# Three z projections by seven block products instead of eight, and norm weights spread by TensorE

## The chip, the cores and the metric

The kernel runs on one core of one Trainium2 chip. The metric is the device time of one execution in microseconds (us), the median of three runs. A profile is one more execution, taken by the hardware profiler. Engines are named as the profile names them: PE is TensorE's matmul, PEld its weight load, DVE is VectorE, ACT ScalarE, POOL GpSimd, and SP the engine whose queue issues every DMA of this kernel.

## What is computed

One layer of a decoder trunk with two token mixers side by side, on 1024 tokens of width 1024. The part that the change touches is the norm of the input and one of the eight parts of the input projection, z_s:

```python
h = rms_norm(x, norm_w)
proj = h @ w_in
q, k, v, z_a, xbc, z_s, dt_raw, gate_logits = jnp.split(proj, SPLIT_POINTS, axis=-1)
...
xbc = jax.nn.silu(causal_depthwise_conv(xbc, conv_w, conv_b))
dt = jax.nn.softplus(dt_raw.astype(jnp.float32) + dt_bias.astype(jnp.float32))
y_s = ssd_chunked(xs, dt, A, Bm, Cm, d_skip)
y_s = gated_group_rms_norm(y_s, z_s, ssd_norm_w)        # y * silu(z), four groups of 512
```

z_s is 2048 wide, 512 columns for each of four groups, and is needed when that group's scan runs.

## The kernel before

**Numbers.** Every fp32 operand of a large matmul is split into a high and a low part of the matmul's own type (ACT copies the high part, DVE or POOL subtracts it from the original), and a product is three matmuls: high x high, high x low, low x high (steps3). hH and hL hold the two parts of the normed input, with its width on the partitions.

**Front.** x comes in eight tiles of 128 tokens. prep_h squares and sums a tile on ACT, takes the root on POOL, scales it on DVE by the root and by the norm's weights (nwb, loaded by two DMAs that write the same row into all 128 partitions), and transposes it on PE; h_evac makes hH and hL. For tokens 512 to 1023, form_evac also makes four sums of quarters of the input (ft), which the seven-product scheme uses.

**The units.** The projection's parts are computed in a fixed order (ORDER1): z of group 0, dt, z of group 1, then the conv and gate parts in pairs, with z of groups 2 and 3 among them, then the attention heads. A conv or gate unit (front_pair) takes the 1024 x 256 weights and the 1024 x 1024 input each as 2x2 blocks and computes the four blocks of the result with seven block products instead of eight; sums of weight blocks are made on POOL (pair_splits), sums of results on DVE (front_sum). Such a product has 12 matmuls of 512 columns. The z units are plain (ssd_proj_z, proj_tok): for each of 8 token tiles, 8 blocks of 128 x 512 weights, three matmuls each, with the input stationary and the weights moving; z_evac puts silu on the result (ACT) and stores it.

**dt.** dt_proj computes 64 result columns, copies them to SBUF (dtraw), transposes them (ptdt) and then runs softplus on DVE and ACT over many small operations (tv).

**What sets the order.** The program is written by a planner (Plan): tasks are Python generators, each instruction has an assumed cost, and what comes next in assumed time is written next. On the chip every engine goes through its own instructions in that order and waits where an operand isn't there; the assumed costs only set the order. Buffers are counted: four raw weight tiles (raws), nine split weight tiles (ws), 16 of 2 KB per partition for everything between (mids), eight PSUM banks (trs). The scan (ssd_chunk) is spread among the units at one chunk per 20 us (PACE) at least. Weights are loaded (w_loads) and split (w_splits) in the order of the units, as far ahead as buffers allow.

Lines of the profile: L199 is every matmul, L208 every transpose, L225 every ACT operation, L233 a two-operand operation on DVE or POOL, L241 one with a scalar, L246 and L250 one-operand ones, L254 a DMA.

Of the kernel before, what the change touches and what calls it, by code (L numbers as in the profile page):

```python
# [8 lines left out]
F32 = mybir.dt.float32  # L9
# [6 lines left out]
P = 128  # L16
# [11 lines left out]
C_B = C_XBC + 2048  # L28
C_C = C_B + 512
C_ZS = 7168  # L30
# [109 lines left out]
def tile_hybrid_layer(ctx: ExitStack, tc: tile.TileContext, x, norm_w, w_in, q_norm_w, k_norm_w,  # L140
# [22 lines left out]
    cv_d = dram.tile([3072, S], F32, name="cv_d")  # L163
    z_d = dram.tile([GROUPS, S, 512], F32, name="z_d")
    t_d = dram.tile([12, 2, P, S], F32, name="t_d")

# [44 lines left out]
    def pe_done():  # L211
        return pl.t + 0.2
# [136 lines left out]

    CONV = (16, 20, 0, 2, 4, 6, 18, 22, 8, 10, 12, 14)  # L350
    ORDER1 = [("z", 0), ("dt", 0), ("z", 1)]
    for i in range(12):
        ORDER1 += [("c", CONV[i])] + ([("g", i - 1)] if i % 2 else [])
        if i in ZF:
            ORDER1.append(("z", ZF[i]))
    FPAIRS = [i for i in ORDER1 if i[0] in "cg"]
    ORDER1.append(("setup", 0))
    for h in range(HEADS):
        ORDER1.append(("h", h))
        if h in ZH:  # L360
            ORDER1.append(("z", ZH[h]))

    wlist = []
    for kind, i in ORDER1:
        if kind in "cg":
            wlist.append(pair_w(w_in, 0, (C_XBC if kind == "c" else C_GATE) + i * P))
        elif kind != "setup":
            wlist += att_w(i) if kind == "h" else wide_w(w_in, C_ZS + i * 512) if kind == "z" else block_w(w_in, KB, C_DT, SH)
# [11 lines left out]
    def w_loads(lo, hi):  # L380
        for i in range(lo, hi):
# [10 lines left out]
            if isinstance(wlist[i], list):  # L392
                ks = yield from pl.get(raws, 4)
                raw = [rpool.tile([P, 4, P], F32, tag="raw", name=f"rawf{i}{q}") for q in range(4)]
                raw_of[i] = (raw, ks, [load(raw[q], wlist[i][q // 2][:, :, q % 2 * P:(q % 2 + 1) * P]) for q in (0, 1, 2, 3)])
                continue
            while i >= len(wlist) - 2 * KB and "filled" not in ready:
# [26 lines left out]
    def w_splits():  # L424
        for i in range(len(wlist)):
# [5 lines left out]
            if isinstance(wlist[i], list):  # L431
                yield from pair_splits(*raw_of.pop(i), "G" if i < NFRONT else "V")
                continue
            k = yield from pl.get(ws)
# [17 lines left out]
    def pair_splits(raw, ks, at, eng):  # L452
# [33 lines left out]
        raws.give(ks[2], t)  # L486
        raws.give(ks[3], max(t, t22))

    def pairs_splits(raw, ks, at):
# [142 lines left out]
    def prep_h(t):  # L632
# [22 lines left out]
        pts = []  # L655
        nt = []
        for i in range(2):
# [400 lines left out]

    cv_at, z_at, ssd_n = {}, {}, {}

    def front_form(f, i):
# [5 lines left out]
    def front_pair(kind, b, last):  # L1067
# [6 lines left out]
        cell = {"kc": (yield from pl.get(mids)), "x": x, "ks": ks}  # L1074
        step = conv_step if kind == "c" else gate_step
        for n, (f, p) in enumerate(ORDER):
# [17 lines left out]
            w_done(ids[n])  # L1094
            pl.spawn(step(b, p, into[p], cell), pe_done())

# [10 lines left out]

    def gate_out(row, h, src, o, k, at):
        yield at
        at = act(o, src, AF.Tanh, at, scale=0.5)  # L1110
        t = at
        yield at
        at = load(gt_d[row * P:(row + 1) * P, h * 512:h * 512 + 512], o, at)
        mids.give(k, at)
        return t

    def gate_step(b, p, ps, cell):
        at = pe_done()
# [3 lines left out]
        elif p == 2:  # L1122
            k = yield from pl.get(mids)
            t = yield from gate_out(b, 0, ps, midt(name="go"), k, at)
            trs.give(kx, t)
        elif p == 4:
            c = cell["c"]
            at = tt(c, c, ps, ALU.add, max(at, cell["u", 7][2]))
            trs.give(ky, at)
            yield from gate_out(b + 1, 0, c, c, cell["kc"], at)  # L1130
        else:
# [5 lines left out]
            if p == 3:  # L1137
                trs.give(kz, at)
            yield from gate_out(b + (p == 5), 1, u, u, k, at)

# [83 lines left out]
    def ssd_core(g):  # L1224
# [16 lines left out]
        need = [(b, h) for b in [16 + g, 20 + g] + list(range(g * 4, g * 4 + 4)) for h in range(2)]  # L1241
        while any(cv_at.get(i, INF) > pl.t for i in need) or any((g, t) not in z_at for t in range(NT)):
            yield pl.t + 0.5
# [513 lines left out]
    def bulk():  # L1757
# [3 lines left out]
        for kind, i in ORDER1:  # L1761
            if kind in "cg":
                yield from front_pair(kind, i, (kind, i) == FPAIRS[-1])
            elif kind in step:
                yield from step[kind](i)
            else:
                yield from dt_proj() if kind == "dt" else att_setup()
        pl.spawn(fill())
# [5 lines left out]

    kn = [mids.take() for _ in range(2)]
    nwb = [midt(name=f"nwb{i}") for i in range(2)]

    def start():
        load_x(0)
        for i in range(2):  # L1780
            load(nwb[i], norm_w[:, i * 512:i * 512 + 512].partition_broadcast(P).rearrange("p a d -> p (a d)"))
        yield from w_loads(0, 4)
# [8 lines left out]
        while len(h_at) < 2 * NT:  # L1791
            yield pl.t + 1.0
        for k in kn:
            mids.give(k, pl.t)

    def rest():
# [35 lines left out]
```

## Time and profile before

| | us |
|---|---|
| median of three runs | 1624.73 (1622.62 to 1625.15) |
| the profiled execution | 1625.04 |
| its span | 1623.3 |
| PE busy in it | 1589.2 (98%) |
| DVE, ACT, POOL busy | 1088.5, 915.1, 706.9 |

The span reaches from the first to the last instruction of the profile; the rest of an execution's time lies around it. Busy time says how long an engine had something in work. An engine that is busy nearly all the time sets the time; what the others do costs only where it waits for them. In the timeline a row has the start, the duration, the engine, the line, the operation, its output and inputs, their size, and a count where rows were merged; a bracket says how long the engine stood idle before and what it waited for. Matmuls overlap: a row's duration is longer than the distance to the next one, and the distance is what counts. In the forms, 128x256 is partitions by columns.

### The profile page before, as it was taken

What the parts mean: (1) busy time and instruction counts of PE and PEld (TensorE: products, weight loads), DVE (VectorE), ACT (ScalarE), POOL (GpSimd) and SP (SyncE); (2) the same over time, 40 slices, a digit from 0 to 9 for tenths busy, and PEclk for the clock granted to TensorE, in tenths of its full rate; (3) what the DMA queues carried; (4) which work ended last, traced back from release to release, by engine and by line L of the source; (5) the groups of instructions that cost most, each with busy time, mean ns of one, the idle gap of its engine ahead of it and who ended that gap; (6) DMA issues with size and microseconds to landing.
All of it is one profiled execution on the core that took longest, in us unless ns stands there. A gap on an engine that the chain in (4) does not pass through costs nothing.

```text
span 1623.3 us, 24344 instructions
## 1 busy us (share of the span) xinstructions
PE 1589.2 (98%) x8010; PEld 1330.2 (82%) x8010; DVE 1088.5 (67%) x2011; ACT 915.1 (56%) x2215; POOL 706.9 (44%) x847
## 2 busy tenths in 40 slices
PE   7999999999999999999989999999999999999999
PEld 5788888888788888887878888887887888888887
DVE  7836567537782576876767777876556577798831
ACT  7534447445563475786766777776666565352220
POOL 4315445334542543546475746464756433323000
PEclk9999999999999999999999999999999999999999
DMA  6213343533453461425163432433426397698941
GB/s 210 92 55 105 112 145 111 168 101 114 125 168 107 121 183 61 131 79 182 40 207 128 145 90 85 120 101 103 155 80 206 99 310 253 207 340 254 317 153 65
DMA packets 223804, 236.47 MB, mean 146 GB/s; under 512 B 15285, under 2 KB 155326, under 8 KB 223678
## 3 DMA queue, kind: packets, MB, share of 16 engines
q1 hardware_dynamic: 223678, 234.93, 45.6%
q8 instruction: 63, 1.03, 0.3%
q14 instruction: 63, 0.52, 0.1%
HBM read 164.48 MB, written 70.39 MB: 145 GB/s over the span
## 4 chain that ended last, share of the span: by engine, by line
PE 73%; DVE 3%; ACT 2%; POOL 2%; DMA 2%; issue 1%; SPq 0%; POOLq 0%; DVEq 0%; ACTq 0%
PE pma L199 18%; PE py L199 6%; PE pmz L199 5%; PE po L199 5%; PE pO L199 4%; PE pz L199 4%; PE px L199 4%; PE sc L199 4%; PE av L199 4%; PE fYc L199 3%; PE fXc L199 2%; PE pg L199 2%; PE pa L208 2%; PE fZc L199 2%; PE fYg L199 1%; PE pS L199 1%
## 5 line engine op out<-in xcount | busy, mean ns | idle before, releaser
L199 PE MATMUL pma<-w,hH 128*128 128x512 f32 x1024 | 345.2, 405 | 6.0 <-POOL w L233 5.4
L199 PEld LDWEIGHTS pma<-w,hH 128*128 128x128 f32 x1024 | 188.6, 189 | 40.9 <-POOL w L233 6.6
L199 PE MATMUL pma<-w,hL 128*128 128x512 f32 x512 | 206.8, 404 | 0.0
L199 PE MATMUL pmz<-w,hH 128*128 128x512 f32 x512 | 164.1, 398 | 0.7 <-ACT hH L225 0.7
L233 POOL TENSOR_TENSOR rawf<-rawf,rawf 128x512 f32<-128x512 f32 x54 | 71.6, 1326 | 166.4 <-DVE wp L233 87.8
L225 ACT ACTIVATE p<-p,nm 128x256 f32<-128x256 f32 (+7 forms) x128 | 98.6, 773 | 33.6 <-DVE nm L831 32.9
L225 ACT ACTIVATE w<-raw 128x512 fp32r<-128x512 f32 (+1 forms) x122 | 75.1, 626 | 75.0 <-DMA raw<-in_w_in_dram 28.7
L199 PEld LDWEIGHTS pmz<-w,hH 128*128 128x128 f32 x512 | 96.5, 190 | 20.6 <-ACT hH L225 1.1
L199 PEld LDWEIGHTS pma<-w,hL 128*128 128x128 f32 x512 | 96.8, 189 | 16.4
L233 POOL TENSOR_TENSOR w<-raw,w 128x512 fp32r<-128x512 f32 (+1 forms) x38 | 51.3, 1351 | 134.5 <-ACT w L225 120.7
L199 PE MATMUL fYc<-ft,wp 128*128 128x512 f32 x432 | 106.5, 392 | 0.7 <-DVE fu L233 0.7
L199 PE MATMUL pmz<-w,hL 128*128 128x512 f32 x256 | 101.4, 396 | 0.0
L199 PEld LDWEIGHTS fYc<-ft,wp 128*128 128x128 f32 x432 | 81.1, 189 | 17.9 <-DVE fu L233 1.1
L225 ACT ACTIVATE wp<-rawp 128x512 fp32r<-128x512 f32 x72 | 44.2, 626 | 84.1 <-POOL rawp L233 23.9
L233 DVE TENSOR_TENSOR wp<-rawf,wp 128x512 fp32r<-128x512 f32 x72 | 59.1, 837 | 34.7 <-ACT wp L225 34.7
L233 DVE TENSOR_TENSOR w<-raw,w 128x512 fp32r<-128x512 f32 (+1 forms) x84 | 65.1, 782 | 23.5 <-ACT w L225 23.3
L225 ACT ACTIVATE ab<-ab,nac 128x128 f32<-128x128 f32 x256 | 78.4, 392 | 1.7 <-POOL ab L1234 1.5
L199 PEld LDWEIGHTS av<-v,at 128*128 128x128 f32 x576 | 72.8, 191 | 6.5 <-ACT at L225 2.6
L265 POOL TENSOR_TENSOR rs<-rs,mhalf 128x4 f32<-128x4 f32 (+1 forms) x71 | 75.4, 1062 | 5.9
L225 ACT ACTIVATE wp<-rawf 128x512 fp32r<-128x512 f32 x108 | 65.9, 626 | 20.0 <-POOL rawf L233 16.4
L199 PE MATMUL av<-v,at 128*128 128x128 f32 x576 | 75.1, 275 | 1.7 <-ACT at L225 1.7
L831 DVE CUSTOM_DVE_ANT_0 p<-sc,maskb 128x512 f32<-128x512 f32 (+3 forms) x128 | 72.1, 584 | 6.2 <-PE sc L199 3.9
(299 smaller groups left out, 4217.8 us busy)
## 6 DMA issues: line engine op xcount, KB each, us to landing
raw<-in_w_in_dram SPq DMA_DIRECT2D x104, 256.0 KB, 3.6
rawf<-in_w_in_dram SPq DMA_DIRECT2D x72, 256.0 KB, 3.7
ab<-act_d SPq DMA_DIRECT2D x32, 512.0 KB, 4.9
cv_d<-cv SPq DMA_DIRECT2D x48, 256.0 KB, 2.1
t_d<-ts SPq DMA_DIRECT2D x24, 512.0 KB, 3.1
z_d<-zs SPq DMA_DIRECT2D x32, 256.0 KB, 2.0
xr<-cv_d SPq DMA_DIRECT2D x32, 256.0 KB, 3.0
zc<-z_d SPq DMA_DIRECT2D x32, 256.0 KB, 3.0
```

The source lines that it names most:

```text
L199: nc.tensor.matmul(o, lhsT=lhsT, rhs=rhs, start=start, stop=stop, **kw)
L208: nc.tensor.transpose(out=o, in_=i, identity=ident if idn is None else idn)
L225: nc.scalar.activation(o, i, f, **kw)
L233: (nc.vector if eng == "V" else nc.gpsimd).tensor_tensor(out=o, in0=a, in1=b, op=op)
L265: nc.gpsimd.tensor_tensor(out=dst, in0=dst, in1=mhalf[:, 0:cols], op=ALU.pow)
L831: nc.vector.tensor_tensor_reduce(out=p[:, j:e], in0=sc[i][:, 0:e - j], in1=maskb[:, S - n + j:S - n + e], scale=-1.0, scalar=nms[i - 1] if ...
```

## The change

z of groups 1, 2 and 3 is computed with seven products of 2x2 blocks too; group 0 stays plain. The new unit (tok_unit) keeps z's layout, tokens on the partitions: the input's blocks are stationary, four tiles of 128 tokens each, and the weights' blocks, 128 x 256, move. A weight block has two tiles (kp) with two blocks of 128 rows each; so a product has 2 x 4 x 2 x 3 matmuls of 256 columns. Two token tiles share a PSUM bank, and each of the three accumulators (x, y, z) has two banks. Results are summed by DVE into 128 x 512 tiles, get silu on ACT and are stored with two tokens tiles each. tok_splits makes the sums of the weights on POOL and the splits on ACT, DVE and POOL; it takes four raw tiles and four of the shared ones (mids) for one unit.

The order of the units is now a string, with z2 ahead of c4 (before, behind g4) and z3 ahead of c8 (before, behind g8). PACE is 21 instead of 20. The norm's weights are loaded as two rows of one partition; a matmul with a column of ones (K = 1) spreads each over 128 partitions into a PSUM bank, which it keeps until all of x is scaled.

```diff
-PACE = 20
+PACE = 21
...
-ZF, ZH = {5: 2, 9: 3}, {}
+FRONT_ORDER = "z0 d0 z1 c16 c20 g0 c0 c2 g2 z2 c4 c6 g4 c18 c22 g6 z3 c8 c10 g8 c12 c14 g10"
+PLAIN = (("z", 0),)
...
+            if isinstance(wlist[i], tuple) and len(wlist[i]) == 8:
+                ks = yield from pl.get(raws, 4)
+                raw = [rpool.tile([P, 2, 256], F32, tag="raw", name=f"rawt{i}{q}") for q in range(4)]
+                at = [load(raw[q], wlist[i][q]) for q in range(4)]
+                km = yield from pl.get(mids, 4)
+                raw += [midt([P, 2, 256], name=f"rawt{i}{q}") for q in range(4, 8)]
+                at += [load(raw[q], wlist[i][q]) for q in range(4, 8)]
...
+    def tok_splits(raw, ks, km, at):
+
+        a11, a21, a12, a22 = [[raw[q], raw[4 + q]] for q in range(4)]
...
+        for kp in range(2):
+            yield t0[kp]
+            t3.append(tt(s3[kp], a11[kp], a21[kp], ALU.subtract, t0[kp], "G"))
+            t1.append(tt(a21[kp], a21[kp], a22[kp], ALU.add, t0[kp], "G"))
+        u11 = yield from split(a11, t0, "V")
+        for kp in range(2):
+            t2.append(tt(a11[kp], a21[kp], a11[kp], ALU.subtract, max(t1[kp], u11[kp]), "G"))
+        yield from split(a11, t2, "V")
+        u12 = yield from split(a12, t0, "V")
+        for kp in range(2):
+            t4.append(tt(a12[kp], a12[kp], a11[kp], ALU.subtract, max(t2[kp], u12[kp]), "G"))
...
+        t = yield from split(s3, t3, "G")
...
+        t = yield from split(a21, t1, "V")
...
+        t = yield from split(a22, t0, "G")
...
+        t = yield from split(a12, t4, "G")
...
+        while "nwb" not in ready:
+            yield pl.t + 0.1
...
+    def tok_unit(kind, g, last):
+
+        ids = w_next(14)
...
+        for n, (f, p) in enumerate(ORDER):
+            for b in range(2 * ((into[p], 0) not in ps)):
+                k = yield from pl.get(trs, first=True)
+                ps[into[p], b] = (trt(f"t{into[p]}{kind}{g}{b}"), k)
+            for kp in range(2):
+                yield from w_need(ids[2 * n + kp])
...
+                for j in range(4):
+                    b = j // 2
+                    while kp == 0 and p in BEFORE and (("c22", b) if p == 3 else (BEFORE[p], b)) not in cell:
+                        yield pl.t + 0.1
+                    o = ps[into[p], b][0][:, j % 2 * 256:j % 2 * 256 + 256]
+                    for kk in range(2):
+                        hf = front_form(f, 2 * kp + kk)
+                        yield from steps3(o, [a[:, j * P:(j + 1) * P] for a in hf], (wt[:, 0, kk], wt[:, 1, kk]),
+                                          kp + kk == 0 and p in (1, 6, 5) and j % 2 == 0, kp + kk == 2, skip_group_check=True)
+                    if kp and j % 2:
+                        pl.spawn(tok_step(kind, g, p, b, ps[into[p], b], cell), pe_done())
...
-    nwb = [midt(name=f"nwb{i}") for i in range(2)]
+    nwr = [midt([1, 512], name=f"nwr{i}") for i in range(2)]
+    nwb = [trt(f"nwb{i}") for i in range(2)]
...
+    def norm_rows(t):
+        yield t
+        for i in range(2):
+            mm(nwb[i], one, nwr[i], True, True)
+        ready["nwb"] = pe_done()
...
-            load(nwb[i], norm_w[:, i * 512:i * 512 + 512].partition_broadcast(P).rearrange("p a d -> p (a d)"))
+            t = load(nwr[i], norm_w[:, i * 512:i * 512 + 512])
+        pl.spawn(norm_rows(t), t)
```

Three places show what the change does to the order. The first is PE between dt (pdt; ptdt are its transposes) and z of group 1 (pmz before, txz after). Before:

```order
L199 MATMUL pdt_780<-hH,w_693 64x512
L199 MATMUL pmz_809<-w_705,hH 128x512 x2
L199 MATMUL pmz_809<-w_705,hL 128x512
L199 MATMUL pmz_809<-w_715,hH 128x512 x2
L199 MATMUL pmz_809<-w_715,hL 128x512
L199 MATMUL pmz_809<-w_724,hH 128x512 x2
L199 MATMUL pmz_809<-w_724,hL 128x512
L199 MATMUL pmz_809<-w_791,hH 128x512 x2
L199 MATMUL pmz_809<-w_791,hL 128x512
L208 MATMUL ptdt<-ident,dtraw_739 128x64 x4
L208 MATMUL ptdt<-ident,dtraw_740 128x64 x4
```

After:

```order
L203 MATMUL pdt_787<-hH,w_696 64x512
L212 MATMUL ptdt<-ident,dtraw_730 128x64 x4
L212 MATMUL ptdt<-ident,dtraw_731 128x64 x4
L203 MATMUL txz_807<-wt_827,hH 128x256 x2
L203 MATMUL txz_807<-wt_827,hL 128x256
L203 MATMUL txz_807<-wt_827,hH 128x256 x2
```

The transposes of dt stood behind four weight tiles of z and now stand ahead of z's first matmul.

The second place is DVE at the same point, where dtraw is dt's copy out of PSUM, tv its softplus, and w or wt a split of z's weights for group 1. Before:

```order
L250 COPY dtraw_740<-pdt_780 64x512
L233 TENSOR_TENSOR w_799<-raw_770,w_799 128x512
L233 TENSOR_TENSOR w_818<-raw_785,w_818 128x512
L233 TENSOR_TENSOR tv_841<-ptdt,dtb 128x256
L233 TENSOR_TENSOR tv_841<-ptdt,tv_841 128x256
L241 SCALAR_TENSOR_TENSOR tv_841<-tv_841 128x256
L233 TENSOR_TENSOR w_849<-raw_826,w_849 128x512
L246 TENSOR_SCALAR tv_842<-tv_841 128x256
L1002 RECIPROCAL tv_842<-tv_842 128x256
```

After:

```order
L254 COPY dtraw_731<-pdt_787 64x512
L237 TENSOR_TENSOR tv_820<-ptdt,dtb 128x256
L237 TENSOR_TENSOR tv_820<-ptdt,tv_820 128x256
L245 SCALAR_TENSOR_TENSOR tv_820<-tv_820 128x256
L237 TENSOR_TENSOR wt_827<-rawt_758,wt_827 128x512
L250 TENSOR_SCALAR tv_821<-tv_820 128x256
L1074 RECIPROCAL tv_821<-tv_821 128x256
L237 TENSOR_TENSOR tv_821<-tv_821,tv_820 128x256
L237 TENSOR_TENSOR tv_821<-tv_821 128x256
L237 TENSOR_TENSOR wt_831<-rawt_766,wt_831 128x512
```

Weight splits that stood ahead of the softplus now stand inside it, the first behind three of its operations and the second behind four more and the reciprocal's input from ACT.

The third place is the start on DVE, where x is scaled by nwb, w is a split of z0's weights and hL the low part of the first tokens. Before:

```order
L241 SCALAR_TENSOR_TENSOR ss<-ss 128x1
L241 SCALAR_TENSOR_TENSOR x_122<-x_122,rs,nwb_118 128x512
L241 SCALAR_TENSOR_TENSOR x_122<-x_122,rs,nwb_119 128x512
L233 TENSOR_TENSOR w_147<-raw_127,w_147 128x512
L233 TENSOR_TENSOR w_155<-raw_129,w_155 128x512
L233 TENSOR_TENSOR hL<-ph_149,hH 128x4x128
```

After:

```order
L245 SCALAR_TENSOR_TENSOR ss<-ss 128x1
L245 SCALAR_TENSOR_TENSOR x_128<-x_128,rs,nwb_122 128x512
L245 SCALAR_TENSOR_TENSOR x_128<-x_128,rs,nwb_123 128x512
L237 TENSOR_TENSOR w_153<-raw_133,w_153 128x512
L237 TENSOR_TENSOR w_158<-raw_135,w_158 128x512
L237 TENSOR_TENSOR w_166<-raw_137,w_166 128x512
L237 TENSOR_TENSOR hL<-ph_160,hH 128x4x128
```

One more split of weights now stands ahead of the first hL.

## Rows read from the trace of the kernel before

**Rows 1.** The page's first part: engine, busy us, share of the span, instructions.
```profile
PE 1589.2 (98%) x8010; PEld 1330.2 (82%) x8010; DVE 1088.5 (67%) x2011; ACT 915.1 (56%) x2215; POOL 706.9 (44%) x847
```

**Rows 2.** The page's fifth part: groups; busy us, mean ns, then idle before.
```profile
L199 PE MATMUL pmz<-w,hH 128*128 128x512 f32 x512 | 164.1, 398 | 0.7 <-ACT hH L225 0.7
L233 POOL TENSOR_TENSOR rawf<-rawf,rawf 128x512 f32<-128x512 f32 x54 | 71.6, 1326 | 166.4 <-DVE wp L233 87.8
...
L199 PE MATMUL pmz<-w,hL 128*128 128x512 f32 x256 | 101.4, 396 | 0.0
```

**Rows 3.** The chain that ended last: start us, us, work and its instruction count.
```profile
305.28 15.45 PE pmz L199 x68
...
1532.88 87.36 PE po L199 x408
```

**Rows 4.** Timeline of the last output tile on PE: start us, us, instruction.
```profile
1615.39 0.88 PE L199 MATMUL po<-w,hH 128*128 128x256 f32 x6
...
1616.11 0.88 PE L199 MATMUL po<-w,hL 128*128 128x256 f32 x6
```

**Rows 5.** Timeline of the first 18 us: SP's issue, DVE and PE.
```profile
1.69 0.90 SPq L254 DMA_DIRECT2D nwb<-in_norm_w_dram  x2
...
6.76 0.75 DVE L241 SCALAR_TENSOR_TENSOR x<-x,rs,nwb 128x512 f32<-128x512 f32 x1 [1.54 <-DMA nwb<-in_norm_w_dram]
...
11.66 0.63 PE L199 MATMUL pmz<-w,hL 128*128 128x512 f32 x1
...
12.94 0.63 PE L199 MATMUL pmz<-w,hL 128*128 128x512 f32 x1
...
17.54 0.40 PE L199 MATMUL pmz<-w,hL 128*128 128x512 f32 x1
```

**Rows 6.** Timeline, scaling of x by norm weights (DVE) and a transpose behind it.
```profile
26.84 1.40 DVE L241 SCALAR_TENSOR_TENSOR x<-x,rs,nwb 128x512 f32<-128x512 f32 x2
...
34.74 2.76 DVE L241 SCALAR_TENSOR_TENSOR x<-x,rs,nwb 128x512 f32<-128x512 f32 x2
...
37.64 0.63 PE L208 MATMUL ph<-ident,x 128*128 128x128 f32 x4 [0.87 <-DVE x L241]
```

**Rows 7.** Timeline around dt's end and the start of z of group 1.
```profile
68.20 4.51 SPq L254 DMA_DIRECT2D raw<-in_w_in_dram  x5
...
71.00 0.63 ACT L225 ACTIVATE w<-raw 128x512 fp32r<-128x512 f32 x1 [1.40 <-DMA raw<-in_w_in_dram]
...
74.28 0.63 PE L199 MATMUL pmz<-w,hH 128*128 128x512 f32 x2
74.48 0.68 DVE L250 COPY dtraw<-pdt 64x512 f32<-64x512 f32 x1 [1.45 <-PE pdt L199]
...
77.12 0.71 PE L208 MATMUL ptdt<-ident,dtraw 64*128 64x64 f32 x8
...
77.86 0.42 DVE L233 TENSOR_TENSOR tv<-ptdt,dtb 128x256 f32<-128x256 f32 x1 [1.50 <-PE ptdt L208]
...
79.12 0.69 DVE L233 TENSOR_TENSOR w<-raw,w 128x512 fp32r<-128x512 f32 x1
```

**Rows 8.** Timeline of DVE alone, what dt's softplus does next.
```profile
81.02 0.29 DVE L246 TENSOR_SCALAR tv<-tv 128x256 f32<-128x256 f32 x1 [1.22 <-ACT tv L225]
...
84.06 1.27 DVE L246 TENSOR_SCALAR tv<-tv 128x256 f32<-128x256 f32 x1
```

**Rows 9.** Timeline of PE alone, a wait amid the conv units.
```profile
419.23 3.62 PE L199 MATMUL pO<-xdt,ab 128*128 128x64 f32 x16 [2.50 <-DVE cv L241]
```

**Rows 10.** Windows of 5 us there: busy us of PE, PEld, DVE, ACT, POOL, then clock, DMA.
```profile
415.00:420.00 5.00, 2.50 (x12) 1.91 (x11) 5.00 (x10) 2.25 (x5) 3.76 (x3) 0.93 0.38 116
420.00:425.00 5.00, 5.00 (x20) 4.52 (x20) 2.77 (x5) 1.06 (x2) 0.00 (x0) 0.50 0.85 220
```

**Rows 11.** Windows of 50 us, same columns.
```profile
300.00:350.00 50.00, 50.00 (x238) 41.71 (x237) 15.45 (x26) 24.10 (x46) 12.21 (x13) 1.00 0.40 124
...
400.00:450.00 50.00, 47.40 (x210) 39.08 (x209) 38.29 (x59) 28.73 (x56) 26.27 (x23) 0.93 0.45 134
```

More of the change, by code (lines that the diff above doesn't have):

```diff
@@ L348, in pair_w @@
                 for q in range(2)]
[L350 to L356, printed above, removed]
+    ORDER1 = []
+    for e in FRONT_ORDER.split():
+        ORDER1.append((e[0], int(e[1:])))
+    FPAIRS = [i for i in ORDER1 if i[0] in "cgazv" and i not in PLAIN]
     ORDER1.append(("setup", 0))
@@ L432, in w_splits @@
                 yield from pair_splits(*raw_of.pop(i), "G" if i < NFRONT else "V")
+                continue
+            if isinstance(wlist[i], tuple) and len(wlist[i]) == 8:
+                yield from tok_splits(*raw_of.pop(i))
                 continue
@@ L1129, in gate_step @@
             trs.give(ky, at)
-            yield from gate_out(b + 1, 0, c, c, cell["kc"], at)
+            yield from gate_out(b + 1, 0, c, c, cell["kc"], at, how)
         else:
@@ L1138, in gate_step @@
                 trs.give(kz, at)
-            yield from gate_out(b + (p == 5), 1, u, u, k, at)
+            yield from gate_out(b + (p == 5), 1, u, u, k, at, how)
+    def tok_unit(kind, g, last):
+        ids = w_next(14)
+        ps = {}
+        into = {1: "x", 6: "y", 2: "x", 7: "y", 5: "z", 4: "y", 3: "z"}
+        cell = {}
+        for n, (f, p) in enumerate(ORDER):
+            for b in range(2 * ((into[p], 0) not in ps)):
+                k = yield from pl.get(trs, first=True)
+                ps[into[p], b] = (trt(f"t{into[p]}{kind}{g}{b}"), k)
+            for kp in range(2):
+                yield from w_need(ids[2 * n + kp])
+                if f[0] == "t":
+                    while any(("formed", t) not in ready for t in range(4, NT)):
+                        yield pl.t + 0.2
+                    at = max(ready["formed", t] for t in range(4, NT))
+                    if at > pl.t:
+                        yield at
+                wt = wts[ids[2 * n + kp]]
+                for j in range(4):
[9 more added lines that the diff above has]
+                        pl.spawn(tok_step(kind, g, p, b, ps[into[p], b], cell), pe_done())
+                w_done(ids[2 * n + kp])
+            if last and f[0] == "t":
+                for part in range(2):
+                    for kp in range(2):
+                        bigs.give(forms_t[f, part, kp][1], pl.t + 0.1)
@@ L1241, in ssd_core @@
         need = [(b, h) for b in [16 + g, 20 + g] + list(range(g * 4, g * 4 + 4)) for h in range(2)]
-        while any(cv_at.get(i, INF) > pl.t for i in need) or any((g, t) not in z_at for t in range(NT)):
+        while any(cv_at.get(i, INF) > pl.t for i in need) or any(z_at.get((g, t), INF) > pl.t for t in range(NT)):
             yield pl.t + 0.5
@@ L1773, in bulk @@
         yield from final()
-    kn = [mids.take() for _ in range(2)]
-    nwb = [midt(name=f"nwb{i}") for i in range(2)]
+    kn, kb_ = [mids.take() for _ in range(2)], [trs.take() for _ in range(2)]
+    nwr = [midt([1, 512], name=f"nwr{i}") for i in range(2)]
+    nwb = [trt(f"nwb{i}") for i in range(2)]
+    one = const.tile([1, P], F32, name="one")
+    nc.gpsimd.memset(one, 1.0)
+    def norm_rows(t):
+        yield t
+        for i in range(2):
+            mm(nwb[i], one, nwr[i], True, True)
+        ready["nwb"] = pe_done()
     def start():
@@ L1792, in start @@
             yield pl.t + 1.0
-        for k in kn:
+        for k, b in zip(kn, kb_):
             mids.give(k, pl.t)
+            trs.give(b, pl.t)
     def rest():
```

120 lines of the change are left out of this document (107 added, 13 removed).

## The prediction

> **What bounds the kernel now.** I read the engine totals first. TensorE (PE) is busy for 1589.2 of the 1623.3 us of the span [rows 1], so 34.1 us are left in which it stands; the reader is to see that no other engine comes near (DVE 67%). Next I looked at how fast PE goes while busy. The chain of waits has a piece of z's second plain unit in which 68 matmuls of 512 columns take 15.45 us, 0.2272 us each [rows 3]; the last stage takes 87.36 us for 360 matmuls of 512 and 48 of 256 columns. So PE is bound by the matmuls it is given, and the time follows their number and columns wherever the operands are ready. Last I read the timeline at the three places where the change moves work: the first 18 us [rows 5], the end of the stage that makes x ready [rows 6], and the end of dt [rows 7]. The clock column shows what a wait of PE can cost beyond itself [rows 9, 10].
>
> **The change part by part.** The sum is made against the profiled execution: 1625.04 us, of which 1623.3 are span. The median of the runs, 1624.73, lies 0.3 below it.
>
> *Matmuls.* A plain unit of z has 8 token tiles x 8 blocks x 3 = 192 matmuls of 512 columns; the whole is 512 + 256 = 768 for four groups [rows 2]. The new unit has 7 products x 2 weight tiles x 4 token tiles x 2 x 3 = 336 of 256 columns. The shape 128x256 with a new stationary tile each time stands in the last output tile: six in 0.72 us, from 1615.39 to 1616.11 [rows 4], so 0.12 us each. With it the last stage gives (87.36 - 48 x 0.12) / 360 = 0.2267 us for 512 columns [rows 3]. One unit: 192 x 0.2267 = 43.5 before, 336 x 0.12 = 40.3 after. Three units: **-9.6 us**, all on the path, since PE is. An eighth of the columns goes, but each matmul has 0.0133 us that doesn't depend on columns (2 x 0.12 - 0.2267), and there are 144 more of them per unit.
>
> The Trainium skill ("TensorE: Matmul & The Clock Gate", Back-to-back issue gap) puts the gap of warm matmuls at N/2.4 + 2.5 ns. That is 215.8 ns for 512 columns and 109.2 for 256; an estimate from this page is 3 x (41.4 - 36.7) = 14.2 us saved. The rows above, 226.7 and 120 ns, don't agree with it.
>
> *z of group 1 directly behind dt.* This is what I expect to cost most. Before, three weight tiles of this unit were split while z0 ran, and its first matmul stands at 74.28, right behind dt's last [rows 7]; the transposes of dt come four tiles later, at 77.12, and nobody waits for them. After, PE has the transposes directly behind dt, and on DVE three operations of dt's softplus stand ahead of the first weight split, and five more (one waits for an exponential on ACT) ahead of the second. DVE works in this order, so PE's second matmul of z waits for them. In the frame of before: the copy of dt's second half starts 0.20 after PE's end and takes 0.68 (74.48 to 75.16); four of the eight transposes, half of 0.71 and their latency, end by some 75.75; the three softplus operations take 79.12 - 77.86 = 1.26, the split 0.69 [rows 7]. That is 77.8 for PE's second matmul, 3.5 after 74.28, of which 0.72 (transposes, which cost this before too) and 0.12 are work: 2.7 lost. The second split starts 84.06 - 77.86 = 6.2 after the softplus began [rows 7, 8], at 82.0, and ends at 82.7; PE is through with the first weight tile at 77.8 + 23 x 0.12 = 80.6 and one matmul further: 2.0 lost. Together **+4.7 us**. The loads don't set this: the burst of eight stands behind z0's last store on SP as the five of before did, issued from 68.20 with the first in use at 71.00 [rows 7]. The third tile needs POOL's chain of five operations, 1.33 each [rows 2], from about 73 to 80, and a split on DVE that ends near 85; PE wants it at 85.5, so I count nothing there. Bounds: 0, if DVE gets to the splits in time, and 4.7 + 2.9 by the next item.
>
> *The clock.* At 416.7 to 419.2 PE waited 2.50 us [rows 9], and then the granted clock was 0.93 and 0.50 of full in two windows of 5 us (0.50 is 1.2 of 2.4 GHz) [rows 10]: 0.35 + 2.5 = 2.9 us lost behind a wait of 2.5. The wait at z1 is as long. But at half speed the first weight tile takes 23 x 0.21 = 4.9 and ends where the second split does, so that the fall only costs what is left of it: I take **+0.5**, bounds 0 and 2.9.
>
> *The norm's weights.* Two loads of 256 KB become two rows and two matmuls. DVE's first scaling of x waited 1.54 us for the load [rows 5]; the row must still pass a matmul of one partition, fp32, ahead of the first transposes. PE's third matmul, at 11.66, waits for DVE's hL, and the change puts one more weight split (0.69, [rows 7]) ahead of that hL; the earlier scaling is used up there: 0, bounds -1 and +1. From 11.66 to 12.94 three matmuls take 1.28, twice the later pitch, and by 17.54 they are full speed [rows 5]; if the matmuls that now come first bring full speed 3 us sooner, 1.4 is saved. With the weights in PSUM the scaling of x no longer reads two SBUF operands. Beside POOL's sums, two of them took 2.76 instead of 1.40 [rows 6], and a transpose waited 0.87 for one. I take **-0.9**, bounds -2.4 and +1 (two of eight PSUM banks are held until x is done).
>
> *Work beside PE.* Each new unit has 8 POOL sums and on POOL 6 splits, 14 x 1.33 = 18.6 us of POOL [rows 2] in 40, on ACT 6 more copies, on DVE some ten more additions from PSUM. The plain unit of group 2 ran while DVE was busy 15.45 of 50 us, conv units with 38.29 [rows 11]; a gate or conv pair has the same density of splits and PE waited little. The loads for the units of groups 2 and 3 stand a whole unit ahead of use. I take 0; bounds -2 and +6, one more loss like that of rows 9 and 10 (2.5 + 2.9) at the upper end. The other pace (21 for 20 us between chunks of the scan) and z2 and z3 three units sooner move work that isn't last to end: 0.
>
> Sum: -9.6 + 4.7 + 0.5 - 0.9 = -5.3, so 1625.04 - 5.3 = 1619.7; as a median, 0.3 less: **1619.4**.
>
> **The rivals.** *No wait at z1.* If the first splits of group 1 come in time, 4.7 + 0.5 stay: 1614.2. Against it: the order of DVE, and that the softplus can't start before dt's second half is copied.
> *Eaten up.* The wait at z1 with the whole fall of the clock (+2.4 more than I took) and one more loss of PE amid conv units (+2 to 5): 1623 to 1627, no change. For it: the front lost 2.6 us of PE and 0.07 x 50 = 3.5 us of clock in the one window 400 to 450 [rows 11], and its orders are all new.
> *Slower: POOL's chain rules the new units.* The third weight tile of a unit hangs on five POOL operations, 6.6 us, behind the last of the loads. If the loads of groups 2 and 3, which wait for four raw buffers at once and then four more of the shared ones, land after their units start, each begins with a wait like z1's, 4.7 + 2.9 = 7.6. Two of them give 1634.6; the gain is gone when each loses 2.7. Against it: those loads stand one unit ahead.
> *Short matmuls without a fixed part.* If 256 columns took half of 512's 0.2267, 0.1133, then 3 x 336 x 0.0067 = 6.7 more are saved: 1612.7. [rows 4] speaks against it. (The page named above goes part of this way, 4.6 us.)
>
> **How the numbers follow.** A difference under 0.2% (3.25 us) is about what can't be told from no change here. Forecast, 1616 to 1622: 0.52. No wait at z1: 0.13; short matmuls: 0.02. Eaten up: 0.22. Slower: 0.11. The range takes in the first four: 1612 (no wait at z1 and -2.4 at the start) to 1627. Faster by over 0.2% (under 1621.5): 0.47 + 0.15 = 0.62. Within: 0.05 + 0.21 = 0.26. Slower (over 1628): 0.12.
>
> **What would show it.** Right: the matmuls of 256 columns in z follow each other at 0.12; about 18 us or less of POOL per unit; a wait of PE for DVE's weight split right behind dt's transposes, then a second one some 3 us on; no wait at the start of z of groups 2 and 3; front shorter by about 5 us where the attention projection begins, and the rest of equal length. Wrong: a pitch over 0.125 (which takes 5 us), waits for POOL inside units, or a change behind that point larger than 3 us.

## The result, and the profile after

The changed kernel takes 1612.17 us (median of four runs, 1608.32 to 1613.28) where the kernel before, run beside it, takes 1623.67 (1620.62 to 1625.15): a ratio of 0.9927, 95% interval 0.9904 to 0.9951, so 11.5 us less. Run again on another occasion it took 1610.31, ratio 0.9924 (0.9911 to 0.9937). The prediction was 1619.4, in a range of 1612 to 1627: the direction was right and the time stands at the range's lower edge. The forecast change was -5.3 and the measured one is more than twice that. The experiments below show where it came from: about half (6.3 us) from the new places and pace, which the sum had at zero, and most of the rest (4.9) from the norm's rows, which it had at 0.9. The term that carried the sum, z's products, gave at most 1.8 in this kernel, which is less than its runs scatter, and nothing but losses in three neighbours of it.

The page's first part of the changed kernel (engine, busy us, share of the span, instructions), the answer to [rows 1]:

```profile
PE 1576.5 (98%) x8446; PEld 1339.2 (83%) x8446; DVE 1129.9 (70%) x2049; ACT 925.8 (58%) x2237; POOL 753.0 (47%) x882
```

The profiled execution took 1608.32, its span 1606.2. PE is busy 12.7 us less, DVE 41.4 and POOL 46.1 more. The timeline of PE at the start (start us, us, instruction, idle before), against [rows 5]:

```profile
4.09 3.75 PE L203 MATMUL nwb<-nwr,one 1*128 1x512 f32 x4 [4.09 <-DMA nwr<-in_norm_w_dram]
...
9.57 1.22 PE L203 MATMUL pmz<-w,hH 128*128 128x512 f32 x2
11.09 0.50 PE L203 MATMUL pmz<-w,hL 128*128 128x512 f32 x1 [0.30 <-DVE hL L237]
11.43 0.62 PE L203 MATMUL pmz<-w,hH 128*128 128x512 f32 x2
11.89 0.39 PE L203 MATMUL pmz<-w,hL 128*128 128x512 f32 x1
...
64.28 0.39 PE L203 MATMUL pdt<-hH,w 128*64 128x512 f32 x1
...
120.29 0.40 PE L203 MATMUL fXc<-hH,wp 128*128 128x512 f32 x1
```

The same three places before (z0's first matmul, dt's first, the first of a conv unit):

```profile
10.64 1.22 PE L199 MATMUL pmz<-w,hH 128*128 128x512 f32 x2 [0.75 <-ACT hH L225]
...
66.90 0.39 PE L199 MATMUL pdt<-hH,w 128*64 128x512 f32 x1
...
120.52 0.39 PE L199 MATMUL fXc<-hH,wp 128*128 128x512 f32 x1
```

The norm's rows occupy PE for 3.75 us while nothing else is there to do; z0's first matmul stands at 9.57 (10.64 before). dt begins at 64.28, 2.62 us earlier than before (66.90). Next, the start of z of group 1, first on PE, then on DVE and on POOL, against [rows 7, 8]:

```profile
72.98 0.38 PE L203 MATMUL txz<-wt,hH 128*128 128x256 f32 x1
76.35 0.58 PE L203 MATMUL txz<-wt,hH 128*128 128x256 f32 x1 [2.98 <-DVE wt L237]
...
81.16 0.39 PE L203 MATMUL txz<-wt,hH 128*128 128x256 f32 x1 [0.43 <-DVE wt L237]
```
```profile
74.01 0.62 DVE L245 SCALAR_TENSOR_TENSOR tv<-tv 128x256 f32<-128x256 f32 x1
74.55 1.74 DVE L237 TENSOR_TENSOR wt<-rawt,wt 128x512 fp32r<-128x512 f32 x1
...
80.42 0.69 DVE L237 TENSOR_TENSOR wt<-rawt,wt 128x512 fp32r<-128x512 f32 x1
```
```profile
74.43 1.32 POOL L237 TENSOR_TENSOR rawt<-rawt,rawt 128x512 f32<-128x512 f32 x1
```

PE's second matmul waits 2.98 us for the first split, which DVE reaches behind three operations of dt's softplus, as forecast. The split itself took 1.74 us, the later one 0.69: a sum on POOL ran from 74.43 to 75.75, and the split ended 0.54 behind it. (The Trainium skill, "SBUF — State Buffer", section "SBUF: two separate sides", says that a DVE operation with two SBUF inputs and a GpSimd operation that reads SBUF exclude each other for the whole of the one that starts first; these rows agree, 1.74 for 0.69.) In z of group 2 the pitch is as taken:

```profile
236.35 0.40 PE L203 MATMUL txz<-wt,hH 128*128 128x256 f32 x2
236.59 0.28 PE L203 MATMUL txz<-wt,hL 128*128 128x256 f32 x1
236.71 0.40 PE L203 MATMUL txz<-wt,hH 128*128 128x256 f32 x2
```

Three matmuls in 0.36 us, 0.12 each, and neither z of group 2 (234.56) nor of group 3 (413.63) begins with a wait.

**Two stages.** To see where the 17 us between the two profiled spans lie, I cut both at the start of the attention projection (pma) and at the output projection (po). Windows of before and of the changed kernel: span of the window, its length, then busy us (count) of PE, PEld, DVE, ACT, POOL, PE's granted clock, DMA share, GB/s.

```profile
60.00:597.84 537.84, 533.29 (x2460) 440.24 (x2459) 329.51 (x537) 276.40 (x521) 222.73 (x190) 0.99 0.40 122
597.84:1532.71 934.87, 918.93 (x4918) 777.52 (x4917) 686.11 (x1366) 587.33 (x1594) 453.94 (x618) 1.00 0.50 160
```
```profile
60.00:588.33 528.33, 519.22 (x2876) 449.28 (x2874) 363.04 (x570) 288.52 (x542) 269.26 (x221) 1.00 0.41 126
588.33:1515.67 927.34, 916.13 (x4923) 775.89 (x4922) 693.72 (x1364) 585.89 (x1595) 456.20 (x621) 1.00 0.50 161
```

Attention begins 9.5 us earlier, of which 2.6 stand at dt's start already. But the stage from there to the output projection, which the change doesn't touch, is 7.5 us shorter too, and the prediction had named a change of more than 3 us there as a sign that it is wrong. Its matmuls are the same; what went is waiting (15.9 us before, 11.2 after) and a fall of the clock (2.9 us, none after).

### The profile page after: what moved, and what is told of

It reads as the page before. It is cut to its first block, busy times and chain, and to the rows that moved or that the text cites. A ratio compares the mean times of both kernels' runs of the same rounds, so it can differ in the third digit from the quotient of the medians.

```text
span 1606.2 us, 25359 instructions
## 1 busy us (share of the span) xinstructions
PE 1576.5 (98%) x8446; PEld 1339.2 (83%) x8446; DVE 1129.9 (70%) x2049; ACT 925.8 (58%) x2237; POOL 753.0 (47%) x882
## 4 chain that ended last, share of the span: by engine, by line
PE 88%; ACT 4%; POOL 2%; DVE 2%; issue 1%; DMA 1%; SPq 0%; DVEq 0%; ACTq 0%; POOLq 0%
PE pma L203 17%; PE fYc L203 6%; PE py L203 6%; PE po L203 5%; PE fXc L203 4%; PE pz L203 4%; PE px L203 4%; PE sc L203 4%; PE pO L203 4%; PE fZc L203 4%; PE av L203 3%; PE tyz L203 3%; PE fYg L203 3%; PE tzz L203 2%; PE pg L203 2%; PE txz L203 2%
## 5 line engine op out<-in xcount | busy, mean ns | idle before, releaser
L229 ACT ACTIVATE w<-raw 128x512 fp32r<-128x512 f32 (+1 forms) x98 | 60.7, 628 | 55.7 <-PE po L203 24.6
L237 POOL TENSOR_TENSOR w<-raw,w 128x512 fp32r<-128x512 f32 (+1 forms) x30 | 41.8, 1394 | 96.9 <-ACT w L229 83.1
L935 POOL TENSOR_TENSOR rec<-s,mone 128x1 f32<-128x1 f32 x64 | 37.7, 590 | 87.0 <-ACT p L229 86.9
L237 POOL TENSOR_TENSOR rawp<-rawp,rawp 128x512 f32<-128x512 f32 x36 | 53.0, 1486 | 53.5 <-DVE wp L237 45.1
L237 DVE TENSOR_TENSOR wp<-rawf,wp 128x512 fp32r<-128x512 f32 x72 | 55.4, 784 | 23.0 <-ACT wp L229 23.0
L203 PE MATMUL sc<-kk,qh 128*128 128x512 f32 (+3 forms) x192 | 66.5, 352 | 2.2 <-DVE kk L237 2.2
L237 DVE TENSOR_TENSOR w<-raw,w 128x512 fp32r<-128x512 f32 (+1 forms) x68 | 58.6, 874 | 12.4 <-ACT w L229 12.2
```

The costliest lines, as they stand in the source:

```text
L203: nc.tensor.matmul(o, lhsT=lhsT, rhs=rhs, start=start, stop=stop, **kw)
L229: nc.scalar.activation(o, i, f, **kw)
L237: (nc.vector if eng == "V" else nc.gpsimd).tensor_tensor(out=o, in0=a, in1=b, op=op)
L935: nc.gpsimd.tensor_tensor(out=rec, in0=sums[1], in1=mone, op=ALU.pow)
```

## The experiments

All were timed beside the kernel before (its medians 1623.0 to 1623.8), so medians of two kernels may differ by some 1 us from this alone. "Places" means the places of z of groups 2 and 3 in the order of units.

**The changed kernel again.** No edit.

> The changed kernel once more, for a second profile and a narrower interval. In the first profiles the projection of attention began 9.5 us earlier than before (588.33 for 597.84), and the end came 17.1 us earlier, though the medians differ by 11.5. If the order of instructions decides what is lost (theory A), attention begins at 588 to 589 again and the stage from there to the products at 1287.19 takes 697 to 701 us again, for 706.4 before. If that stage differs from run to run for no reason of the change (theory B), it takes 702 to 706 here, while the front is the same. Time 1609 to 1614 either way.

1610.31. The stage from attention's start to the products, named in the expectation, took 699.7 us (591.79 to 1291.44), as theory A has it, and the whole stage to the output projection 928.13: the shorter stage came again. But attention began at 591.79, not at 588 to 589, which neither theory had. The waits of PE over 1.5 us stand in the same places, all but the one at z1 (3.52 for 2.98) with the same lengths. What differs is what follows them. PE's wait in the first and in the second profile, then windows of 5 us of the first and of the second:

```profile
391.33 0.65 PE L212 MATMUL py<-ident,xn 128*128 128x128 f32 x4 [3.32 <-ACT xn L229]
```
```profile
392.40 1.11 PE L212 MATMUL py<-ident,xn 128*128 128x128 f32 x4 [3.32 <-ACT xn L229]
```
```profile
390.00:395.00 5.00, 3.67 (x18) 3.13 (x19) 4.21 (x10) 4.97 (x10) 2.52 (x2) 1.00 0.23 74
395.00:400.00 5.00, 5.00 (x23) 4.13 (x22) 3.66 (x6) 1.57 (x3) 2.93 (x2) 1.00 0.59 194
```
```profile
390.00:395.00 5.00, 2.60 (x8) 2.23 (x9) 5.00 (x11) 4.97 (x11) 2.79 (x3) 0.61 0.27 92
395.00:400.00 5.00, 5.00 (x17) 4.00 (x16) 1.52 (x4) 2.63 (x5) 2.92 (x2) 0.71 0.52 174
```

The same wait of 3.32 us is followed by full clock in one execution and by half speed in the other.

**dt's softplus later.**

```diff
-        pl.spawn(dt_rest(raw, km), at)
+        pl.spawn(dt_rest(raw, km), at + 14.0)
```

> dt's transposes and softplus are handed to the planner 14 us later, so that all eight weight splits of group 1 that DVE makes stand ahead of the softplus. Nothing else is edited. If the wait at the start of z of group 1 costs what the trace shows (2.98 + 0.43 us of waits, some 1.3 of half speed), this gives 4 to 5 us: ratio to the changed kernel 0.997, some 1607 to 1608, unless the sums of weights on POOL are late next (the third weight tile would wait about 1 us). Rival: the wait is hidden work that is lost again elsewhere, or the new order behind it loses as much: no gain, 1612.

1608.54 (1608.01 to 1609.15), ratio to before 0.9909 (0.9897 to 0.9922): 1.8 us below the changed kernel, and the lowest median of all that ran. That is less than half of the 4 to 5 expected, and the two intervals overlap. The first conv unit starts 53.2 us behind dt's start, 56.0 in the changed kernel: 2.8 won there. What is left are mainly two waits: 1.26 us behind the copy of dt's second half, which stayed ahead of the split on DVE, and 0.74 us where the split waits for ACT's copy and that for POOL's sum:

```profile
73.80 0.39 PE L203 MATMUL txz<-wt,hH 128*128 128x256 f32 x1 [1.26 <-DVE wt L237]
...
81.06 3.01 PE L203 MATMUL tyz<-wt,ft 128*128 128x256 f32 x23 [0.74 <-DVE wt L237]
```

**All z units plain**, order, pace and rows as changed.

```diff
-PLAIN = (("z", 0),)
+PLAIN = tuple(("z", i) for i in range(4))
```

> The changed kernel with z of all four groups plain: the order of units, the pace and the norm's rows stay as changed. The z units' gain alone should be 9.6 us of matmuls less 4.9 at the start of group 1, so this one takes 4 to 6 us more than the changed kernel (1616 to 1618) if theory A holds: the start gave 2.6 and the order and the pace gave the rest of what the forecast lacks. If the seven products themselves gave more than their matmuls, it is 9 to 10 us slower than the changed kernel (1621 to 1622, only the start's 2.6 below the kernel before).

1612.06, ratio 0.9937 (0.9922 to 0.9951). Neither expectation holds: without any seven products the kernel is at most 1.8 us slower than with them. Even that isn't shown: these runs took 1609.97 to 1616.43, and the nine of the changed kernel, both occasions taken together, 1608.32 to 1613.28 with a median of 1611.33. Its window from 60 us to attention:

```profile
60.00:586.80 526.80, 526.58 (x2445) 434.95 (x2443) 331.88 (x536) 274.53 (x521) 226.82 (x189) 1.00 0.40 125
```

PE stands for 0.2 us in 527. The seven products take PE's work out of this stage and put waits into it; attention begins later with them (588.33) than without (586.80).

**The norm's rows alone**, in the kernel before (nwr, one, norm_rows and the two PSUM banks as in the change; z, order and pace as before).

> The kernel before with the norm's weights alone changed: two rows, spread by matmuls into two PSUM banks. In the changed kernel dt began 2.62 us earlier (64.28 for 66.90). If that is all this part does, 2.6 us faster than before (ratio 0.9984, 1621), dt at 64.3. My forecast had 0.9 for this. Rival: the planner's order behind it moves too, and the losses of the later stages (2.5 us of wait and a fall of the clock at 415 to 430, 6 us in 830 to 850) come or go by it: anything from 1615 to 1626, and the front to the attention's start other than 595.2.

1618.43, ratio 0.9966 (0.9952 to 0.998): 4.9 us less than before, more than the 2.6 expected. dt starts at 64.43, 2.47 us earlier than before, as expected. Windows from z0's first matmul to dt's first, before, in this kernel and in the changed one:

```profile
10.64:66.90 56.26, 54.15 (x250) 43.38 (x251) 51.59 (x84) 40.16 (x84) 26.52 (x28) 1.00 0.38 130
```
```profile
10.23:64.43 54.20, 53.51 (x252) 43.41 (x251) 48.75 (x84) 39.98 (x85) 24.76 (x27) 1.00 0.38 134
```
```profile
9.57:64.28 54.71, 52.48 (x252) 41.63 (x251) 49.23 (x82) 37.81 (x80) 24.03 (x27) 1.00 0.35 118
```

In this kernel z0 starts 0.41 earlier, PE stands for 0.69 us of the window instead of 2.11 (1.42 less), and it is busy 0.64 less. The changed kernel reaches dt at the same time by another road: z0 starts 1.07 earlier, PE stands as long as before (2.23), and it is busy 1.67 less, since z0's matmuls reach their full pitch at 11.4, where here the half-speed pitch lasts past 14.9 (before, past 15.5). The clock column reads 1.00 in all three; the pitch shows it. Here three matmuls take 1.28 us at 13.62, in the changed kernel 0.69 at 11.43:

```profile
13.62 1.05 PE L199 MATMUL pmz<-w,hH 128*128 128x512 f32 x2
14.47 0.63 PE L199 MATMUL pmz<-w,hL 128*128 128x512 f32 x1
14.90 0.63 PE L199 MATMUL pmz<-w,hH 128*128 128x512 f32 x1
```

Of the 2.47 us, 1.0 is lost again between dt and the first conv unit, where PE waits 0.64 us in z of group 1. The attention stage is 2.6 us shorter than before (932.3 for 934.9), so the rival holds too. The waits among the conv units are those of before: the one of [rows 9] is there with its 2.50 us.

```profile
417.73 3.03 PE L199 MATMUL pO<-xdt,ab 128*128 128x64 f32 x16 [2.50 <-DVE cv L241]
```

**The seven products in the old order** (old places, pace 20).

```diff
-PACE = 21
+PACE = 20
-FRONT_ORDER = "z0 d0 z1 c16 c20 g0 c0 c2 g2 z2 c4 c6 g4 c18 c22 g6 z3 c8 c10 g8 c12 c14 g10"
+FRONT_ORDER = "z0 d0 z1 c16 c20 g0 c0 c2 g2 c4 c6 g4 z2 c18 c22 g6 c8 c10 g8 z3 c12 c14 g10"
```

> The changed kernel with the old places of z of groups 2 and 3 and the old pace of 20: against the kernel with the norm's rows alone (1618.4) only the seven products of groups 1 to 3 are added. By the terms of the forecast (9.6 of matmuls less 5.2 at the start of group 1) 1614. If the seven products add waits among their neighbours wherever they stand, as they seem to in the new order (all plain 1612.1, seven 1610.3: 1.8 instead of 4.4), 1616 to 1618, with PE waits over 2 us between 100 and 590 that the kernel with the rows alone doesn't have.

1622.81, ratio 0.9995 (0.9984 to 1.0006): 4.4 us more than the rows alone, outside both expectations. The waits are there, longer than thought:

```profile
295.02 5.49 PE L203 MATMUL fYg<-ft,wp 128*128 128x512 f32 x12 [3.53 <-DVE fu L237]
...
470.11 3.64 PE L203 MATMUL pO<-xdt,ab 128*128 128x64 f32 x16 [7.17 <-DVE cv L245]
```
```profile
468.76 1.20 DVE L237 TENSOR_TENSOR ab<-ab,pc 128x1024 f32<-128x1024 f32 x1
```
```profile
465.00:470.00 5.00, 0.00 (x0) 0.00 (x0) 5.00 (x9) 1.11 (x2) 2.54 (x2) 0.81 0.86 213
470.00:475.00 5.00, 4.89 (x20) 4.63 (x21) 1.46 (x4) 1.15 (x2) 2.55 (x2) 0.50 0.50 165
```

In the first window PE does nothing while DVE, without a gap, works off conv sums (cv) and four operations of the scan that stand ahead of the scan's ab. The bracket names cv, but ab itself ends at 469.96, and PE goes on 0.15 later, at half speed.

**Places and pace apart**, all z units plain: new places with pace 20, then old places with pace 21.

> All four groups plain, norm's rows, new places of z of groups 2 and 3, pace 20. Between the rows alone (1618.4, old places, pace 20) and all plain in the new order at pace 21 (1612.1) lie 6.3 us. If the places did it, this is 1612 and the front has none of the waits at 295, 385 and 417 (0.9, 0.7, 2.5 us and the fall of the clock behind the last). If the pace did it, 1618 and the waits are there.

1610.28, ratio 0.9919 (0.9905 to 0.9933). PE waits 0.2 us between 60 us and attention; the three waits are gone:

```profile
60.00:586.06 526.06, 525.83 (x2441) 434.33 (x2439) 333.21 (x535) 273.52 (x519) 225.79 (x189) 1.00 0.41 125
```

> All four groups plain, norm's rows, old places of z of groups 2 and 3, pace 21: the other half of the 6.3 us. If the pace did it, 1612; if the places did it, 1618, with the waits at 295, 385 and 417. If both give the full gain, or neither, there is no such cause: every new order draws its own waits, and the sum of waits of PE behind 60 us, not the place of any unit, goes with the time.

1613.01, ratio 0.9937 (0.9923 to 0.995). The waits at 294, 383 and 416 are there (0.89, 0.71, 2.50), and yet it is 5.4 us faster than the rows alone at pace 20, and the profiles differ most in the attention stage, 925.9 for 932.3 (rows alone, then this kernel):

```profile
596.33:1528.65 932.32, 917.83 (x4919) 775.84 (x4918) 685.92 (x1366) 586.30 (x1593) 453.17 (x619) 1.00 0.50 160
```
```profile
593.09:1518.96 925.87, 916.33 (x4919) 776.54 (x4917) 683.67 (x1366) 587.50 (x1594) 451.31 (x618) 1.00 0.50 162
```

Either edit alone gives 5 to 8 us and both together no more (6.3), so their gains don't add. That is the outcome for which the expectation had said that the total has no single such cause and goes with the sum of PE's waits. The stages tell more: the new places empty the front of these waits, and the pace changed what is lost in attention.

**Group 1 plain**, the rest as changed (`PLAIN = (("z", 0), ("z", 1))`).

> The changed kernel with group 1 plain too, so that only groups 2 and 3 have seven products. Group 1 then costs 3.2 us more of matmuls and loses no 3.4 us of waits and 1.3 of half speed: by these terms 1.9 us less than the changed kernel, 1608.4, and the first conv unit starts at 118.0 to 118.5 (120.3 in the changed kernel, 118.0 with all plain). Rival: the order behind it is drawn anew, so that waits elsewhere move the time by more than this, 1606 to 1614.

1613.29, ratio 0.994 (0.9927 to 0.9954). The first conv unit starts 53.6 us behind dt's start instead of 56.0, as expected. But from there to attention it takes 470.9 where the changed kernel takes 468.0, so that the 2.4 are lost again ahead of attention, and the attention stage takes 932.1 where the changed kernel's takes 927.3. The rival holds.

**The seven products in the other two orders:** new places with pace 20, old places with pace 21.

> The changed kernel with pace 20. With this run and the next the seven products are compared with plain z four times: so far 4.4 us slower (old places, pace 20: 1622.8 for 1618.4) and 1.8 faster (new places, pace 21: 1610.3 for 1612.1); plain with new places and pace 20 is 1610.3. If the seven products carry a steady cost beside PE (some 5 us, the load that they put on DVE and POOL), this is 1608 to 1612, within 2 us of plain. If it is the chance of each order, anything from 1603 to 1615, and the sum of PE's waits and of its fall of the clock goes with the time, while PE's work at full clock from 60 us to the start of attention is again 518 us (526 for plain).

1623.95, ratio 1.0011 (0.9997 to 1.0024), above both expectations: one number, 20 for 21, takes back the whole gain of the change. The front is that of the changed kernel (530.1 us, the same waits at 392 and 409, 3.2 for 3.0 at z1), with 518.6 us of work at full clock as expected. The attention stage takes 940.2, with 15.1 us of waits and 9.0 lost to the clock, all of it between 905 and 940, behind two waits, for a load of the scan and for ACT:

```profile
906.43 0.83 PE L212 MATMUL px<-ident,xr 128*128 128x128 f32 x4 [1.97 <-DMA xr<-cv_d]
...
924.01 3.56 PE L203 MATMUL av<-v,at 128*128 128x128 f32 x16 [2.58 <-ACT at L229]
```
```profile
910.00:915.00 5.00, 4.91 (x24) 4.61 (x23) 1.37 (x3) 1.96 (x9) 3.09 (x5) 0.50 0.51 151
915.00:920.00 5.00, 5.00 (x22) 4.60 (x22) 3.88 (x7) 2.25 (x5) 1.21 (x2) 0.50 0.08 28
```
```profile
590.13:1530.30 940.17, 925.02 (x4923) 784.75 (x4921) 681.95 (x1364) 585.27 (x1595) 454.66 (x621) 0.99 0.49 159
```

> The changed kernel with the old places of z of groups 2 and 3 and pace 21; plain in this order is 1613.0. By a steady cost beside PE 1611 to 1614. By the chance of each order 1606 to 1620. In both cases work at full clock of 518 us between 60 us and the start of attention, and 3.4 us of PE's waits at the start of z of group 1.

1621.94, ratio 0.9997 (0.9987 to 1.0007), above both expectations (1611 to 1614, 1606 to 1620); work at full clock is 519.3 us, near the 518 expected, and PE waits 3.7 us at z1.

**dt's softplus later, at pace 20 and 22.**

> dt's softplus 14 us later and pace 20. At pace 21 the later softplus gave 1608.5 for 1610.3. If only the start of group 1 counted, this would be 1.8 below the changed kernel with pace 20. It is also a try at a better version: 1604 to 1612.

1616.05, ratio 0.9954 (0.9938 to 0.997), outside the range, and 7.9 us below the changed kernel with pace 20, not 1.8.

> dt's softplus 14 us later and pace 22: the same edit in a third order, 1604 to 1612. The waits in z of group 1 (1.26 + 0.74 us at pace 21) are the same, since the scan hasn't begun there; what differs from late_dt at pace 21 is the sum of waits and falls of the clock behind 120 us.

1621.14, ratio 0.9988 (0.9976 to 1.0), outside the range again. The first wait at z1 is the same (1.26), the second 0.18 instead of 0.74. The three kernels with the later softplus have the same front (60 us to attention 528.7 to 529.1); the attention stage takes 935.8, 927.3 and 938.7 us at pace 20, 21 and 22.

## Why the prediction was off

The medians as a table, all with the norm's rows:

| places, pace | z plain | z of 3 groups by seven products | difference |
|---|---|---|---|
| old, 20 | 1618.4 | 1622.8 | +4.4 |
| old, 21 | 1613.0 | 1621.9 | +8.9 |
| new, 20 | 1610.3 | 1624.0 | +13.7 |
| new, 21 | 1612.1 | 1610.3 | -1.8 |

In the three losses the intervals of the two ratios to before lie apart. In the last row they overlap, and with all nine runs of the changed kernel the -1.8 is -0.7.

And one profile of each, cut into the front (60 us to attention) and the stage from there to the output projection. "Idle" is the time in which PE had no matmul; "clock" is what the granted clock took, the sum of (1 - clock) x busy over windows of 5 us; "work" is the rest of the front.

| kernel | front | idle | clock | work | attention stage | idle | clock |
|---|---|---|---|---|---|---|---|
| before | 537.8 | 4.6 | 3.2 | 530.1 | 934.9 | 15.9 | 2.9 |
| rows alone (old, 20) | 536.3 | 5.1 | 3.0 | 528.2 | 932.3 | 14.5 | 1.1 |
| plain, old, 21 | 533.1 | 4.6 | 1.4 | 527.1 | 925.9 | 9.6 | 1.0 |
| plain, new, 20 | 526.1 | 0.2 | 0.0 | 525.8 | 930.7 | 10.7 | 3.3 |
| plain, new, 21 | 526.8 | 0.2 | 0.0 | 526.6 | 933.2 | 14.1 | 1.3 |
| seven, old, 20 | 543.5 | 15.9 | 9.7 | 517.9 | 925.8 | 9.6 | 0.0 |
| seven, old, 21 | 541.9 | 16.0 | 6.6 | 519.3 | 930.4 | 11.3 | 3.5 |
| seven, new, 20 | 530.1 | 9.2 | 2.4 | 518.6 | 940.2 | 15.1 | 9.0 |
| changed (seven, new, 21) | 528.3 | 9.1 | 1.2 | 518.0 | 927.3 | 11.2 | 0.0 |
| changed, again | 531.8 | 9.7 | 3.7 | 518.5 | 928.1 | 9.7 | 3.4 |

Taken off the profiled execution's time, the four losses (idle and clock of both stages) leave 1594.6 to 1597.3 us in the four plain kernels with the rows and 1586.1 to 1587.2 in the five profiles with seven products. So the products save 7 to 11 us of PE's work in every order, and what spreads the times is how much PE loses beside it: 14 to 24 us in the plain kernels, 21 to 37 in the others.

*Matmuls, -9.6: right within some 1 us.* The mean of work is 526.9 for the four plain kernels with the rows and 518.5 for the five with seven products: 8.4 us less, at a pitch of 0.12. The 262 cycles, 0.109 us at 2.4 GHz, that the Trainium skill ("TensorE: Matmul & The Clock Gate", Back-to-back issue gap) gives as the isolated gap of 256 columns aren't what these matmuls run at.

*The wait at z1, +4.7, and the clock there, +0.5: right in sum, mixed in parts.* From dt's start to the first conv unit the changed kernel takes 56.0 us, before took 53.6: +2.4, and the forecast for this stretch was 5.2 - 3.2 = +2.0. Idle time was 3.8 us where the forecast had 4.7, the clock took 1.2 where it had 0.5. The first wait came out longer (second matmul 4.7 us behind dt's end, not 3.5, because POOL held the split up by 1.05) and the second shorter (0.43, not 2.0, because half speed, from 76.35 to some 78.9, had made PE late). The 2.9 that the prediction read from [rows 10] counts the first window's fall over all 5 us; over the 2.5 in which PE was busy it is 2.7.

*The norm's weights, -0.9: too small by 1.6 at dt's start.* The term had given the earlier scaling of x away again, because one more split stands ahead of hL, and had counted little for scaling from PSUM. Measured are 2.5 at dt's start with the rows alone, more than half of it by removed waits, and 2.6 in the changed kernel, there by the earlier first matmul (1.1) and by full speed sooner (1.7; the bound had 1.4), with no less waiting. That both give the same is chance. Behind dt the rows alone lose 1.0 in z of group 1 and win 2.6 in the attention stage, and their median lies 4.9 below that of before.

*Work beside PE, pace and order, 0 with bounds of -2 and +6: the step that failed.* It was one term for three things, and each of them is larger than the sum of the forecast. First, the new places alone empty the front of the losses that I had read in [rows 9 to 11] and taken as a warning of what new orders bring: 8.1 us of idle and clock with the rows alone, 0.2 with the places. I had seen 2.5 + 2.9 lost at one place and asked only whether another such loss would come, not whether this one would stay. With seven products, too, the front idles less at the new places (9.1 and 9.2 us) than at the old (15.9 and 16.0). Second, the seven products add 9 to 11 us of idle time to the front (0.2 becomes 9.1 to 9.7, 4.6 and 5.1 become 16.0 and 15.9) and 1 to 7 us at half speed: in the changed kernel 3.4 at z1 and 4.9 at 391 and 407, with old places 3.5 and 7.2 at 295 and 470. That eats up the 8.4 of matmuls in every one of the four orders: the front is 1.5 to 5 us longer with seven products at new places, 7 to 9 at old ones. The rival "eaten up" had this mechanism. Third, pace and order move the attention stage between 925.8 and 940.2 us with the same matmuls in it, by waits for POOL, DVE, ACT and loads and by the clock behind them; 21 for 20 makes it shorter in two of the four pairs and longer in the other two. The changed kernel drew 927.3 there, where before takes 934.9 and all plain in the same order 933.2: that alone offsets what its products lose in the front.

So the sum of the changed kernel against before, in profiled spans: -2.6 at dt's start, +2.4 to the first conv unit, -9.3 from there to attention, -7.6 behind it: -17.1. In medians it is -11.5: the changed kernel's profiled execution is the fastest of its four, 3.9 below their median, with a granted clock of 0.999 over the span against 0.995 in the three others, and that of before stands 1.4 above its median.

That the forecast's direction was right is luck: the prediction expected the gain from the products, and it came with the norm's rows and the pair of places and pace that the change brings along. At pace 20 or at old places the same products, with the norm's rows, give no gain over the kernel before.

*What stays open.* Which engine's load makes the front's new waits isn't settled. DVE is busy 31 us more there, POOL 42 (changed against all plain), and the waits name DVE (fu, cv, wt) and ACT (xn); no run took one load away alone with the order kept. Nor is it known why the attention stage idles 9.6 us in one order and 15 in the next; only that the one order that was profiled twice kept its waits. And each row of the second table is one profile, and the front of the changed kernel differs by 3.5 us between its two.

## What to carry to other kernels

When a planner or a table sets the order of every instruction, a change of order is a term of its own, however little the moved work seems to matter: here one step of pace was worth up to 14 us, more than the arithmetic that was saved. List the losses of the trace before and ask of each whether it survives the new order, before asking what new ones come. And test an arithmetic saving in more than one order before crediting it: taking an eighth of the columns off PE gave 8.4 us of work and cost as much or more in waits. The sums that replaced it run on DVE and POOL; that their load makes the waits is likely but wasn't tested by itself.

## What the hardware showed

The same instructions behind the same wait ran at full clock in one execution of the changed kernel and at half speed in another (3.32 us, at 391 and 392). So did the start: in the same two executions, behind the same norm's rows and transposes, z0's matmuls reached full pitch at 11.4 and 12.2. In the nine runs of the changed kernel the granted clock over the span was 0.998 or 0.999 in those of 1608.32 to 1610.31 us and 0.993 to 0.995 in those of 1611.33 to 1613.28: its scatter goes with the clock. In the two that were profiled the clock fell behind the same wait at z1 in both, and behind the waits at 392, 829 and 1087 in the slower one alone.

Two matmuls with one row of stationary operand and 512 fp32 columns took 3.75 us at the start, recorded as four, some 0.9 us apart. PE had nothing else to do then, and DVE's first two scalings of x waited 1.28 and 0.88 us for them, where they had waited 1.54 and 0.46 for the loads before.
